# Two attention heads of one projection started in the same tick instead of two or four ticks apart

## The chip, the cores and the metric

The kernel runs on one core of one Trainium2 chip. The metric is the device time of one execution in microseconds (us). Before the change three runs gave 975.61, 977.11 and 977.17 us, median 977.11 us.

## What is computed

The reference is two transformer blocks for 256 tokens of width 1024, in float32. The first block has two layers: a multi-scale pooling mixer with a SwiGLU feed-forward, then a **differential attention** with eight heads (two score matrices per head, 64 wide, whose softmaxes are subtracted) with another SwiGLU. The second block has a mixer with three branches and a squared-ReLU feed-forward. Two of its branches are attentions with eight heads of width 64, called MoBA and DSA here; the third is a recurrent unit. DSA first lets an indexer select keys. Cut to the two attentions that matter:

```
s = einsum('bhcqd,bhckd->bhcqk', q, k) * 64**-0.5 + bias     # first block, c = 0, 1
p = softmax(where(rel >= 0, s, -inf))
o = (p[:, :, 0] - lam * p[:, :, 1]) @ v ; o = o * rsqrt(mean(o*o) + eps) * g
...
p = softmax(q @ k.T * 64**-0.5 + bias)                       # second block, heads a and b
y = p @ v
```

## The kernel before, in words

All instructions are emitted by one Python program, and each engine executes its own in the order in which they were emitted. A tile is taken from a pool when its first writer runs and goes back when its last reader has run. The pools of PSUM are small (`BANKS`, L169): four banks `acc`, two `mm`, two `tr`. If none is free, the writing instruction waits, and with it all that stands behind it on its engine.

The main work is projections and feed-forward products, split in high and low parts: each product is three matmuls (L318 to L320). A unit of weights (256 columns) comes by DMA as two raw tiles; ScalarE casts each to its high part (L92) and VectorE subtracts for the low part (L101). `Stream.step` emits these: two casts once a unit's room is released, and the subtractions one tick later.

Attention runs beside that work as Python generators in the list of `Side`. A call of `side.tick()` advances each generator by one step (until its next `yield`), in the order of the list, and then calls `Stream.step`. A generator may have a delay in ticks and a list of others that must have ended first. `proj_b` (L342) ticks after the first half of a unit (24 matmuls); `proj_t` (L816) copies the result from PSUM on ScalarE (L821, tile `qk`) after the second half and then ticks. So a projection is two ticks, an odd one in its middle and an even one at its end, and a pair of projections (q and k) is four. The casts of L92 come at even ticks behind the heads' instructions, the subtractions of L101 at odd ticks, also behind them.

The steps of one differential head (`diff_head`, L861, with `softmax`, L827), with letters used below:

- S: four score matmuls of 64 rows (L834) into two `acc` banks; VectorE adds the bias and reduces (L841, four instructions).
- E: four exponentials on ScalarE (L847).
- N: VectorE normalises and subtracts (L866 to L870).
- T: three transposes (L856) into one `tr` bank, copied out by ScalarE (L858).
- O: the value product, three matmuls (L877 to L879) into one `acc` bank; ScalarE squares (L883).
- G: two small instructions on GpSimd (L885, L388).
- D: VectorE scales out of the `acc` bank (L890).
- F: two transposes (L895) into one `tr` bank; ScalarE writes the high part from it (L314) and VectorE the low part from it (L315).

A pair of heads in the second block (`head_pair`, L1086) has six steps: S and E as above, N (L1091, L1094), T twice (six transposes in two `tr` banks, L856, with two copies L858), O (four matmuls of 64 columns, L1104, into one `acc` bank, high part by ScalarE, L1107) and the low part (L1109).

Before the change the eight differential heads are added two at a time after each q and k (L904 to L911): the first starts at the next tick, the second two ticks later. For the last pair the first head's S is run at once (L910), the second waits one tick. After them come the last part of v (`v_last`, L912: two ticks, with the copies L813 from its `mm` bank) and the output product (L914 to L923), whose first accumulators are both `mm` banks.

In the second block `heads_of` (L1116) adds two pairs of heads for MoBA at j = 0, the second four ticks after the first, and at j = 1 two more, each two ticks after the pair of j = 0 with its number has ended. They stand at the front of the list. DSA does the same later, after a masked bias is there. At the first tick of MoBA the indexer (L975) also runs a step, with four score matmuls in two times two `acc` banks.

Of the kernel before, what the change touches and what calls it, by code (L numbers as in the profile page):

```python
# [161 lines left out]
def model_kernel(ctx: ExitStack, tc: tile.TileContext, a: dict, out: bass.AP, stop=None):  # L162
# [16 lines left out]
    def gen(tag="rn", shape=(512,), dt=F32):  # L179
        return sb.tile([P] + list(shape), dt, tag=tag, name=nm(tag), bufs=BUFS[tag])  # L180
# [110 lines left out]
    side = Side(st)  # L291
# [85 lines left out]
    def hidden():  # L377
        return gen("hh", (2, 256), F32R), gen("hl", (2, 256), F32R)
# [427 lines left out]
    def v_last(v):  # L806
        u = st.take()[0]
        b = bank("mm")
        for t in range(2):
            proj_a(b[:, t * 256:(t + 1) * 256], t, u, False)  # L810
            if t:
                for i in range(2):
                    nc.scalar.copy(v[i][:, 768:1024], b[:, i * 256:(i + 1) * 256])  # L813
            side.tick()

    def proj_t():  # L816

        u = st.take()[0]
        b = proj_b(u)
        o = gen("qk", (2, 256))  # L820
        nc.scalar.copy(flat(o), b)  # L821
        side.tick()
        return o
# [79 lines left out]
    heads = []  # L903
    for j in range(4):  # L904
        qT, kT = proj_t(), proj_t()
        hts.append(hidden())
        for i in range(2):
            g = diff_head(qT, kT, i, 2 * j + i, hts[j], v, bias)
            if j == 3 and not i:
                next(g)  # L910
            heads.append(side.add(g, 2 * i if j < 3 else i))  # L911
    v_last(v)  # L912
    gb = bcast(a["ln_mix_g"][1]), bcast(a["ln_mix_b"][1])
    parts = list(zip(hts, st.take(4)))  # L914
# [171 lines left out]
    def head_pair(qT, kT, j, pr, b0, b1, v0, yT):  # L1086
        sx = []
        yield from softmax(qT, kT, j, lambda c, t: (b0, b1)[t](2 * pr + c), sx)
        p, sm = sx
        rc = small(4)  # L1090
        nc.vector.reciprocal(rc, sm)  # L1091
        for t in range(2):
            for c in range(2):
                nc.vector.tensor_scalar_mul(p[c][:, SPAN[t]], p[c][:, SPAN[t]], rc[:, 2 * t + c:2 * t + c + 1])  # L1094
        yield
        pT = [transpose3(p[c]) for c in range(2)]
        yield
        ob = bank("acc")
        for k in range(2):
            for c in range(2):  # L1100
                r = slice(c * 64, (c + 1) * 64)
                vc = slice(v0 + (2 * pr + c) * 64, v0 + (2 * pr + c + 1) * 64)
                q = slice(k * P, T)
                nc.tensor.matmul(ob[r, q], lhsT=v[k][:, vc], rhs=pT[c][:, (0, T)[k]:(T, 384)[k]],  # L1104
                                 start=k == 0, stop=k == 1, skip_group_check=True)
        h, l = yT[0][:, pr % 2], yT[1][:, pr % 2]
        nc.scalar.copy(h, ob[:, 0:T])  # L1107
        yield
        nc.vector.tensor_sub(l, ob[:, 0:T], h.bitcast(F32))  # L1109
# [6 lines left out]
    def heads_of(pairs, j, qT, kT, b0, b1, v0, yT, after=()):  # L1116

        for i in range(2):
            g = head_pair(qT, kT, i, 2 * j + i, b0, b1, v0, yT)
            pairs.append(side.add(g, 2 if j else 4 * i, pairs[i:i + 1] if j else after, True))  # L1120

    def moba(j):
        heads_of(ma, j, proj_t(), proj_t(), lambda h: bias_a[j][:, h % 4, P:T], lambda h: bias_a[j][:, h % 4], 0, yaT[j])

    def dsa(j, after):
        heads_of(d, j, proj_t(), proj_t(), lambda h: bias0[0][:, h], lambda h: bias_b[j][:, h % 4], 512, ybT[j], after)
# [19 lines left out]
    for what, j in MERGE:  # L1146
        u = st.take()[0]
        if what in "ABC":
            b = proj_b(u)
            g = gates[what, j] = gen("gt")  # L1150
# [12 lines left out]
        else:  # L1163
# [3 lines left out]
            g = gates.pop((what.upper(), j))  # L1167
# [60 lines left out]
def build(inputs, stop=None):  # L1228
    import concourse.bacc as _bacc

    nc = _bacc.Bacc("TRN2", target_bir_lowering=False, num_devices=1)
    arrays, args = {}, {}
    for name, v in [(n, inputs[n]) for n in _INS] + list(_constants().items()):
        v = np.ascontiguousarray(v)
        arrays[f"in_{name}_dram"] = v
        args[name] = nc.dram_tensor(f"in_{name}_dram", v.shape, mybir.dt.from_np(v.dtype), kind="ExternalInput").ap()
    out = nc.dram_tensor("out_0_dram", (1, T, D), F32, kind="ExternalOutput").ap()
    with tile.TileContext(nc) as tc:
        model_kernel(tc, args, out, stop)
    return nc, arrays  # L1240
# [8 lines left out]
```

## Time and profile before

| | us |
|---|---|
| runs, median (lowest to highest) | 977.11 (975.61 to 977.17) |
| the profiled execution, its own time | 977.19 |
| its span in the profile | 975.4 |
| TensorE busy | 951.4 (98%) |
| VectorE busy | 597.2 (61%) |
| ScalarE busy | 490.5 (50%) |
| GpSimd busy | 21.6 (2%) |
| chain of waits that ended last: TensorE's share | 89% |

The profile follows one execution. The difference of 1.8 us between its time and its span lies before the first and after the last instruction. TensorE is PE in the rows (PEld its weight loads), VectorE DVE, ScalarE ACT, GpSimd POOL. Matmuls are pipelined, so the time that one takes from the stream is read from start to start, not from its duration. A float32 matmul leaves two records.

### The profile page before, as it was taken

The numbers are of one execution on the slowest core, as the hardware profiler recorded it, in microseconds if no ns is written. First come the engines' busy times: TensorE is split into PE (matmuls) and PEld (weight loads), VectorE is DVE, ScalarE is ACT, GpSimd is POOL, SyncE is SP. The second block draws the span as 40 slices with busy tenths as digits, with TensorE's granted clock in tenths as the row PEclk, the third lists the DMA queues.
The fourth block names the chain that finished last, engine by engine and source line by source line (L and its number), as shares of the span: only waits on it lengthen the run. The fifth ranks groups of instructions, "written<-read, shape, count | busy, mean of one in ns | idle before, by whom it ended". The sixth has DMA issues, their size and how long they took to land.

```text
span 975.4 us, 16057 instructions
## 1 busy us (share of the span) xinstructions
PE 951.4 (98%) x6443; PEld 859.2 (88%) x6443; DVE 597.2 (61%) x985; ACT 490.5 (50%) x813; POOL 21.6 (2%) x44
## 2 busy tenths in 40 slices
PE   6999999999999999999998999999999999999997
PEld 5789999988998789999996999998999978898896
DVE  5774554466676864544458468958755676555454
ACT  3553543345666653433445456669644555344441
POOL 0000000000012000000001000000000000000000
PEclk9999999999999999999999999999999999999999
DMA  6576666556635466676752855443655657565531
GB/s 218 173 257 206 219 212 219 174 163 197 200 130 173 142 204 194 216 251 206 266 180 86 243 180 173 149 125 118 194 172 187 223 172 220 184 221 194 177 108 43
DMA packets 133939, 179.71 MB, mean 184 GB/s; under 512 B 8387, under 2 KB 114140, under 8 KB 133864
## 3 DMA queue, kind: packets, MB, share of 16 engines
q1 hardware_dynamic: 133008, 177.82, 57.0%
q8 instruction: 50, 0.82, 0.3%
q10 hardware_dynamic: 856, 0.87, 0.3%
q14 instruction: 25, 0.20, 0.1%
HBM read 177.51 MB, written 5.79 MB: 188 GB/s over the span
## 4 chain that ended last, share of the span: by engine, by line
PE 89%; DVE 5%; ACT 2%; issue 2%; DMA 1%; POOL 0%; POOLq 0%; DVEq 0%; ACTq 0%
PE mm L318 21%; PE mm L320 20%; PE mm L319 20%; PE acc L320 8%; PE acc L318 8%; PE acc L319 7%; DVE wl L101 2%; PE acc L834 1%; PE acc L1104 1%; PE tr L856 1%; DVE x L412 1%; ACT rn L401 1%; DMA bc<-in_pool_scale_dram 1%; PE tr L396 0%; POOL sm L388 0%
## 5 line engine op out<-in xcount | busy, mean ns | idle before, releaser
L101 DVE TENSOR_TENSOR wl<-raw,wh 128x1024 fp32r<-128x1024 f32 (+1 forms) x314 | 355.1, 1174 | 125.7 <-ACT wh L92 125.4
L92 ACT CAST wh<-raw 128x1024 fp32r<-128x1024 f32 (+1 forms) x314 | 303.2, 1012 | 171.5 <-issue 137.4
L318 PE MATMUL mm<-XTh,wh 128*128 128x256 f32 x1320 | 374.7, 284 | 0.0
L319 PE MATMUL mm<-XTl,wh 128*128 128x256 f32 x1320 | 368.2, 279 | 0.0
L320 PE MATMUL mm<-XTh,wl 128*128 128x256 f32 x1320 | 368.1, 279 | 0.0
L318 PEld LDWEIGHTS mm<-XTh,wh 128*128 128x128 f32 x1320 | 246.7, 187 | 5.9 <-issue 4.0
L319 PEld LDWEIGHTS mm<-XTl,wh 128*128 128x128 f32 x1320 | 247.7, 188 | 1.4
L320 PEld LDWEIGHTS mm<-XTh,wl 128*128 128x128 f32 x1320 | 248.2, 188 | 0.0
L318 PE MATMUL acc<-wh,hh 128*128 128x512 f32 x350 | 139.3, 398 | 0.0
L320 PE MATMUL acc<-wh,hl 128*128 128x512 f32 x350 | 139.0, 397 | 0.0
L319 PE MATMUL acc<-wl,hh 128*128 128x512 f32 x350 | 137.8, 394 | 0.0
L320 PEld LDWEIGHTS acc<-wh,hl 128*128 128x128 f32 x350 | 65.7, 188 | 16.5 <-DVE hl L312 0.4
L319 PEld LDWEIGHTS acc<-wl,hh 128*128 128x128 f32 x350 | 65.7, 188 | 14.4
L318 PEld LDWEIGHTS acc<-wh,hh 128*128 128x128 f32 x350 | 65.7, 188 | 13.7 <-ACT hh L311 0.2
L319 PE MATMUL mm<-wl,XTh 128*128 128x512 f32 (+1 forms) x144 | 53.7, 373 | 1.8 <-DVE wl L101 1.8
L318 PE MATMUL mm<-wh,XTh 128*128 128x512 f32 (+1 forms) x144 | 54.4, 378 | 0.2 <-ACT XTh L311 0.2
L320 PE MATMUL mm<-wh,XTl 128*128 128x512 f32 (+1 forms) x144 | 53.3, 370 | 0.3 <-DVE XTl L312 0.3
L312 DVE TENSOR_TENSOR hl<-rn,hh 128x512 fp32r<-128x512 f32 x30 | 20.8, 692 | 50.1 <-ACT hh L311 50.1
L605 ACT ACTIVATE rn<-mm 128x512 f32<-128x512 f32 x18 | 10.8, 602 | 60.7 <-PE mm L320 60.7
L821 ACT COPY qk<-mm 128x512 f32<-128x512 f32 x22 | 12.9, 588 | 44.0 <-PE mm L320 41.3
L319 PEld LDWEIGHTS mm<-wl,XTh 128*128 128x128 f32 x144 | 27.1, 188 | 8.1 <-DVE wl L101 3.6
L388 POOL TENSOR_TENSOR sm<-sm,mhalf 128x1 f32<-128x1 f32 (+1 forms) x22 | 14.4, 655 | 810.7 <-DVE sm L424 422.6
(208 smaller groups left out, 888.8 us busy)
## 6 DMA issues: line engine op xcount, KB each, us to landing
raw<-in_w_down_dram SPq DMA_DIRECT2D x76, 512.0 KB, 4.5
raw<-in_w_up_dram SPq DMA_DIRECT2D x68, 512.0 KB, 4.2
raw<-in_w_in_dram SPq DMA_DIRECT2D x60, 512.0 KB, 4.6
raw<-in_w_gate_dram SPq DMA_DIRECT2D x36, 512.0 KB, 4.4
raw<-in_w_qkv_dram SPq DMA_DIRECT2D x24, 512.0 KB, 3.6
raw<-in_w_o_dram SPq DMA_DIRECT2D x16, 512.0 KB, 3.7
Rd<-R SPq DMA_DIRECT2D x6, 766.0 KB, 7.0
raw<-in_w_gate_dram SPq DMA_DIRECT2D x16, 256.0 KB, 6.0
```

The source lines that it names most:

```text
L92: self.nc.scalar.copy(h, raw)
L101: self.nc.vector.tensor_sub(l, raw, h)
L312: nc.vector.tensor_sub(l, src, h.bitcast(F32))
L318: nc.tensor.matmul(o, lhsT=lh, rhs=rh, start=first, stop=False)
L319: nc.tensor.matmul(o, lhsT=lh, rhs=rl, start=False, stop=False)
L320: nc.tensor.matmul(o, lhsT=ll, rhs=rh, start=False, stop=last)
L388: nc.gpsimd.tensor_tensor(r2, v, mhalf.to_broadcast([P, n]) if n > 1 else mhalf, ALU.pow)
L401: nc.scalar.activation(gen(shape=(x.shape[-1],)), x, AF.Square, bias=bias, scale=1.0 / 32.0, accum_out=acc_col)
L412: nc.vector.scalar_tensor_tensor(x[:, c], x[:, c], ALPHA, mix, op0=ALU.mult, op1=ALU.add, accum_out=sums[:, h:h + 1])
L605: nc.scalar.activation(s, b, AF.Silu)
L821: nc.scalar.copy(flat(o), b)
L834: nc.tensor.matmul(bs[c][:, SPAN[t]], lhsT=qT[r, j, t * P:(t + 1) * P], rhs=kT[r, j, 0:P * (t + 1)], start=True, stop=True)
```

## The change

In the first block all heads start with delay 0, and for the last q and k both heads run S at once. In the second block both pairs of j = 0 start with delay 0, and both of j = 1 two ticks after both pairs of j = 0 have ended. No instruction is added or removed; only the order changes.

```diff
         for i in range(2):
             g = diff_head(qT, kT, i, 2 * j + i, hts[j], v, bias)
-            if j == 3 and not i:
+            if j == 3:
                 next(g)
-            heads.append(side.add(g, 2 * i if j < 3 else i))
+            heads.append(side.add(g))
     v_last(v)
...
         for i in range(2):
             g = head_pair(qT, kT, i, 2 * j + i, b0, b1, v0, yT)
-            pairs.append(side.add(g, 2 if j else 4 * i, pairs[i:i + 1] if j else after, True))
+            pairs.append(side.add(g, 2 if j else 0, pairs[0:2] if j else after, True))
```

## Rows read from the trace of the kernel before

**Rows 1.** Busy time by engine in the two attention stretches: PE, PEld, DVE, ACT, POOL, clock, DMA.

```profile
245.00:325.00 80.00, 78.63 (x592) 70.88 (x591) 61.20 (x188) 52.51 (x147) 9.45 (x16) 1.00 0.51 166
560.00:705.00 145.00, 143.09 (x1196) 134.28 (x1195) 110.05 (x267) 98.87 (x206) 0.74 (x2) 1.00 0.51 157
```

**Rows 2.** Timeline of PE around the first heads' S: start, us, engine, line, tiles, count.

```profile
251.01 0.28 PE L320 MATMUL mm<-XTh,wl 128*128 128x256 f32 x1
251.21 0.93 PE L834 MATMUL acc<-qk,qk 64*128 64x128 f32 x8
...
252.29 0.28 PE L319 MATMUL mm<-XTl,wh 128*128 128x256 f32 x1
...
257.93 0.93 PE L834 MATMUL acc<-qk,qk 64*128 64x128 f32 x8
```

**Rows 3.** Timeline of PE where a head pair's S meets the indexer.

```profile
578.61 0.93 PE L834 MATMUL acc<-qk,qk 64*128 64x128 f32 x8
579.36 0.60 PE L975 MATMUL acc<-at,qk 64*128 64x256 f32 x4
580.47 0.70 PE L975 MATMUL acc<-at,qk 64*128 64x256 f32 x4 [0.51 <-DVE sm L841]
```

**Rows 4.** Timeline of PE: a head pair's O behind another's S, and an O alone.

```profile
593.29 0.93 PE L834 MATMUL acc<-qk,qk 64*128 64x128 f32 x8
...
594.95 0.39 PE L318 MATMUL mm<-XTh,wh 128*128 128x256 f32 x1
...
701.62 0.87 PE L1104 MATMUL acc<-at,bc 128*64 128x256 f32 x8
702.42 0.39 PE L318 MATMUL mm<-XTh,wh 128*128 128x256 f32 x1
```

**Rows 5.** Timeline of DVE behind the first S: its first reduction, then the subtractions.

```profile
252.17 0.29 DVE L841 CUSTOM_DVE_ANT_0 at<-acc,bias 128x128 f32<-128x128 f32 x1 [2.83 <-PE acc L834]
...
253.29 2.36 DVE L101 TENSOR_TENSOR wl<-raw,wh 128x1024 fp32r<-128x1024 f32 x2
```

**Rows 6.** Timeline of DVE: one head's N, first and last instruction, and one F.

```profile
257.58 0.18 DVE L866 RECIPROCAL sm<-sm 128x4 f32<-128x4 f32 x1 [1.26 <-ACT at L847]
...
258.90 0.48 DVE L870 SCALAR_TENSOR_TENSOR at<-at,sm,at 128x256 f32<-128x256 f32 x1
...
278.38 0.48 DVE L315 SCALAR_TENSOR_TENSOR hl<-tr,sg,hh 128x256 fp32r<-128x256 f32 x1 [0.57 <-ACT hh L314]
```

**Rows 7.** Timeline of ACT: an even tick's copy, the first of one head's E, the casts.

```profile
255.20 0.59 ACT L821 COPY qk<-mm 128x512 f32<-128x512 f32 x1 [4.23 <-PE mm L320]
255.69 0.41 ACT L847 ACTIVATE at<-at,sm 128x128 f32<-128x128 f32 x1
...
257.46 1.98 ACT L92 CAST wh<-raw 128x1024 fp32r<-128x1024 f32 x2
```

**Rows 8.** Timeline of ACT: copies of one pair's T, a table load, the recurrent unit.

```profile
590.39 0.87 ACT L858 COPY at<-tr 128x384 f32<-128x384 f32 x2
...
614.19 1.09 ACT L1023 ACTIVATE rn<-qk,rnn 128x256 f32<-128x256 f32 x2
...
650.25 1.28 ACT L847 ACT_TABLE_LOAD   x1
...
680.98 1.15 ACT L1081 ACTIVATE hh<-qk 128x512 fp32r<-128x512 f32 x2
```

**Rows 9.** Timeline of PE: two waits of the kernel before in these stretches.

```profile
311.29 0.30 PE L856 MATMUL tr<-ident,at 128*128 128x128 f32 x1 [0.85 <-DVE at L870]
...
674.40 1.24 PE L1104 MATMUL acc<-at,bc 128*64 128x256 f32 x8 [0.95 <-ACT at L858]
```

**Rows 10.** Clock after an early wait of PE: timeline of PE, then two windows as in Rows 1.

```profile
17.20 3.64 PE L723 MATMUL acc<-pw,rn 128*128 128x256 f32 x8 [2.33 <-DVE rn L718]
...
17.40:20.70 3.30, 3.30 (x9) 2.45 (x9) 1.54 (x3) 1.10 (x2) 0.15 (x1) 0.50 0.07 24
20.80:30.00 9.20, 7.18 (x37) 5.82 (x36) 7.96 (x12) 4.86 (x6) 0.00 (x0) 1.00 0.46 142
```

## The prediction, made before the changed kernel ran

> **What bounds the kernel.** I read the busy times first: TensorE works 98% of the span, and in the two stretches that the change touches it is busy 78.6 of 80 us and 143.1 of 145 us [rows 1]. So what it does there, and what it would newly wait for, is the time. VectorE is busy 61.2 and 110.1 us of the same stretches, ScalarE 52.5 and 98.9 [rows 1]: two thirds to three quarters, which leaves little for work that comes in bursts. Then I read TensorE's timeline, to price each step of a head from start to start, and last the timelines of VectorE and ScalarE, to see in which order they serve the heads and the weights.
>
> Prices. Between the matmuls that frame S alone pass 1.28 us (251.01 to 252.29), two plain steps among them; from this S to the next pass 6.72 us, 48 plain steps and one S [rows 2]. Both together give a plain step of 0.118 us and an S of 1.04 us. A half projection, 24 steps, is 2.83 us, and two ticks are 5.7 us. The profiled execution took 977.19 us, 0.08 above the median of the runs; I add to the median. About 0.2% (2 us) is what a measurement tells from no change.
>
> **Part 1, what the joins save.** Where other matmuls of 64 rows follow S, they start 0.75 us after it [rows 3], not after the exit that makes S alone cost 1.04. A second S behind a first should cost a little less than 0.75, since its weights are loaded in the shadow of the first: I take 0.66, a gain of 0.38 per join (0.29 by the plain row). Four joins of differential heads: **-1.5**.
> In the second block an S and an O that stand together cost 1.85 us (593.29 to 594.95, and 0.2 at the edges), an O alone 1.0 (701.62 to 702.42, and 0.2) [rows 4]; an O behind an O should be 0.65, like an S. Four pairs before: S, three times S with O, O, so 1.04 + 5.55 + 1.0 = 7.6. After: twice two S (1.70) and two O (1.65), 6.7. Twice -0.9: **-1.8**.
> The rule of the Trainium skill that bears on it is in "TensorEngine Tiling (Array Packing)", Key Properties: a change of tiling mode drains TensorE, so that neighbours of one mode gain. The rows agree, with 0.75 against 1.04. By that rule alone all of the change would be gain, the first rival below.
>
> **Part 2, two S in four `acc` banks.** For the first and the last q and k all four banks are free. For the two between, the order of one tick becomes O, O, S, S: the two O hold a bank each until D, two ticks later, the first S takes the other two, and the second S has none until VectorE has reduced the first. The reductions start 0.96 us after S does (251.21 to 252.17) and take 1.12 (252.17 to 253.29) [rows 2, 5], so the bank is free 2.1 to 2.2 us after the first S began, where the second could have begun at 0.75 [rows 3]. TensorE executes in order: the next half projection stands behind. Two waits of 1.5 with the new entry: **+3.0**. That it waits so is seen where the indexer meets S: 0.51 us until the reduction [rows 3].
>
> **Part 3, F and T in two `tr` banks.** At the end of the second and of the third q and k the order of one tick becomes F, F, T, T (before, F and T of one head each, which just fits). Each F fills a bank that goes back when VectorE has written the low part. Count from x, the end of TensorE's projection at the tick of E. ScalarE: 0.2 until the copy, copy 0.5 (255.20 to 255.69), two E of 1.77 (255.69 to 257.46) [rows 7], so 4.25. The second N starts 0.1 later and takes 1.8 (257.58 to 259.38) [rows 6]: 6.15. Behind it on VectorE stand the tick's two subtractions, 2.36 [rows 5], and only then F's low part, 0.48 [rows 6]: x + 9.0. TensorE arrives after two half projections and the two F (four transposes at the plain step): x + 6.15. The wait is 2.85, twice: **+5.7**. What hid this before is that one head's E, N and F lay two ticks from the other's.
> The first pair's second T waits for its N (x + 6.15 against 5.7 + 0.35): **+0.2**. At the end of the first block the copies of v (L813) come behind two O, two E, and hold the bank that the output product's second half wants: my estimate is **+0.5**. The wait of the last head's T, 0.85 [rows 9], goes: **-0.9**.
>
> **Part 4, four T in two `tr` banks.** Two pairs in step make four T in a tick; the third waits for ScalarE's copy of the first. ScalarE: 0.2, copy 0.5, two E 3.54, the tick's casts 1.98 [rows 7], the next copy of q or k 0.5, one T copied 0.5 (0.87 for two) [rows 8]: x + 7.2. TensorE is there at 5.7 + 0.7. So the bare wait is 0.8; it grows by what else ScalarE does in these two ticks. MoBA first: a table load, 1.28 [rows 8], and the indexer's own work, which is late by about 0.5: 2.6. MoBA second: the recurrent unit's 1.09 [rows 8]: 1.9. DSA first: a table load and about 1 us of the recurrent unit: 3.0. DSA second: 1.15 [rows 8]: 1.9. Together **+9.4**. At MoBA's first tick the indexer, which took two banks freely and two after a wait, now waits for all four: **+0.7**. The wait of O at 674.40, 0.95 [rows 9], goes, since its T are far ahead: **-1.0**.
>
> **The sum.** First block -1.5 + 3.0 + 5.7 + 0.2 + 0.5 - 0.9 = +7.0. Second block -1.8 + 9.4 + 0.7 - 1.0 = +7.3. So 977.1 + 14.3 = 991.4 us, without the clock.
> **The clock.** TensorE's granted clock is 1.00 in both stretches [rows 1]. Early in the run it waited 2.33 us for VectorE, and from then on 0.50 was granted (1.2 of 2.4 GHz) for at least 3.3 us, before 1.00 again [rows 10]. Four of my waits are longer than 2.33 (2.85 twice, 2.6 and 3.0). Half speed for 3.3 us loses up to 1.65; I take 1.5. A fall after two of the four: +3.0, **994.4 us**. The Trainium skill, "TensorE: Matmul & The Clock Gate", in its table "Why this matters for your kernels", asks to avoid idle gaps between bursts of matmuls; by its limit none of my waits is long enough, and the sum would stay 991.4. The early wait speaks against it, and the page is not followed.
> No row of before shows eight such waits in these ticks. From below, the longest wait that it does show there is 0.95 [rows 9]: eight of that are 7.6 in place of 18.1, and the time 981. From above, waits longer by a sixth (+3.0) and four falls (+6.0): 1001. I take the worked-out waits, as the chains are made of measured pieces.
>
> **Rivals.** *Faster, the joins alone.* If the banks come back before TensorE asks (F's low part by x + 6.15 in place of x + 9.0, the T copies by x + 6.4), only the gains stay: -1.5 - 0.9 - 1.8 - 1.0 = -5.2, so 971.9. For it: each join gains by the rows. Against it: VectorE alone would need both the subtractions and a quarter of N out of the way. It decides where a burst of two E is shorter than about 2.3 us in place of 3.5.
> *Shorter waits.* If the casts are not behind the E of these ticks (no room in the weight buffers), the four T waits lose up to 2.0 each and all but vanish, -7.4, and there are fewer falls: 984. Against it: casts follow E in the row [rows 7].
> *No fall of the clock*: 991.4.
> *It does not do what it says.* In two of the four joins of differential heads the two S do not meet in time, because of the bank; that is in the sum.
>
> **Chances.** Forecast 0.50; no fall 0.20; shorter waits 0.18; joins alone 0.08; gains and waits that cancel 0.04. The range 981 to 1001 takes in all but the last two. Faster by over 0.2%: 0.08; within: 0.04; slower: 0.88.
>
> **What would show it.** In the changed profile: eight clusters of S of about 1.7 us, but with a wait on L841 inside two of the differential heads'; in front of T, TensorE idle for VectorE at L315 twice, near 2.6 us, and for ScalarE at L858 four times, 1 to 3 us; VectorE and ScalarE busy as long as before; TensorE's share of busy time down to about 97%; two to four stretches of granted clock 0.50 behind these waits. I am wrong if the waits on L315 and L858 are under 1 us each.

## The result: 992.29 us, and the profile after

The changed kernel takes 992.29 us (median; 991.51 to 993.82), against 977.11 before: a ratio of 1.0164, 95% interval 1.0153 to 1.0175, +15.2 us. The forecast was 994.4, with a range of 981 to 1001. The profiled execution took 992.13 us, its span is 990.3.

Where the time came from is read by three matmuls that stand outside the changed stretches and serve as anchors. L674 runs ahead of the first attention, L962 between the two, and the last of L396 behind the second. The fences give, for each line's matmuls, shape and count, min/median/max duration in ns, and the first and last start in us. First the kernel before:

```profile
L674 PE MATMUL tr<-ident,gt x1: 242/242/242, 239.5 to 239.5; 32*128 32x32 f32 x1
L962 PE MATMUL tr<-ident,at x2: 226/226/226, 564.1 to 564.1; 72*128 72x72 f32 x2
L396 PE MATMUL tr<-ident,rn x32: 270/273/328, 518.3 to 794.9; 128*128 128x128 f32 x32
```

And after:

```profile
L674 PE MATMUL tr<-ident,gt x1: 242/242/242, 237.8 to 237.8; 32*128 32x32 f32 x1
L962 PE MATMUL tr<-ident,at x2: 226/226/226, 570.1 to 570.1; 72*128 72x72 f32 x2
L396 PE MATMUL tr<-ident,rn x32: 270/273/329, 524.3 to 809.8; 128*128 128x128 f32 x32
```

L674 comes 1.7 us earlier, L962 6.0 later, the last transposes 14.9 later. So the start, which the change doesn't touch, gave 1.7 back in this execution (more on that at the end). **The first attention costs +7.7, the second +8.9**, 16.6 together. These two parts are quoted below for every kernel, always as differences to the profile of before.

Now the two stretches after (columns as in [rows 1]), and what TensorE waited for in them (total us, times, longest):

```profile
PE 954.1 (96%) x6443; PEld 863.6 (87%) x6443; DVE 597.5 (60%) x985; ACT 491.3 (50%) x813; POOL 19.1 (2%) x44
...
245.00:335.00 90.00, 82.23 (x593) 73.83 (x591) 62.57 (x188) 54.12 (x152) 7.53 (x17) 0.98 0.48 153
570.00:722.00 152.00, 143.13 (x1177) 134.85 (x1177) 109.34 (x266) 98.00 (x206) 0.74 (x2) 0.98 0.47 141
```

```profile
PE tr L856 <- DVE hl L315: 5.2, 2, 2.6
PE acc L834 <- DVE sm L841: 1.9, 2, 0.9
PE mm L318 <- ACT bc L813: 0.7, 1, 0.7
...
PE tr L856 <- ACT at L858: 8.2, 4, 3.6
PE acc L975 <- DVE sm L841: 0.3, 1, 0.3
PE tr L856 <- DVE at L1094: 0.2, 1, 0.2
```

The first three are the first attention, the rest the second. All but the last 0.2 are waits for a PSUM bank, in the tiles and on the lines that the prediction named; the four for L858 last 3.6, 2.1, 1.6 and 0.9 us, where 1 to 3 was forecast. VectorE and ScalarE are as busy as before (597 and 491 us): no work was added, only waiting. The idle times in these rows sum to 16.5 us.

The two kinds of wait in the first attention, in TensorE's timeline (start, us, then the instruction, and in brackets the idle time before it and its releaser; a transpose leaves one record, so that x6 is the T of two heads and x4 the F of two):

```profile
249.45 1.58 PE L834 MATMUL acc<-qk,qk 64*128 64x128 f32 x16
...
264.63 0.93 PE L834 MATMUL acc<-qk,qk 64*128 64x128 f32 x8
266.50 1.26 PE L834 MATMUL acc<-qk,qk 64*128 64x128 f32 x8 [0.94 <-DVE sm L841]
276.30 0.60 PE L895 MATMUL tr<-ident,at 128*128 128x128 f32 x4
279.53 1.54 PE L856 MATMUL tr<-ident,at 128*128 128x128 f32 x6 [2.64 <-DVE hl L315]
...
297.46 0.60 PE L895 MATMUL tr<-ident,at 128*128 128x128 f32 x4
300.65 0.94 PE L856 MATMUL tr<-ident,at 128*128 128x128 f32 x6 [2.60 <-DVE hl L315]
```

At 249.45, with all `acc` banks free, two S stand in one piece of 1.6 us. At 264.63 two O hold two banks, and the second S stands apart. At 276.30 F fills both `tr` banks and T stops. What held those two banks is seen on VectorE and ScalarE (same columns):

```profile
276.33 0.48 DVE L870 SCALAR_TENSOR_TENSOR at<-at,sm,at 128x256 f32<-128x256 f32 x1
276.73 2.35 DVE L101 TENSOR_TENSOR wl<-raw,wh 128x1024 fp32r<-128x1024 f32 x2
279.00 0.87 DVE L315 SCALAR_TENSOR_TENSOR hl<-tr,sg,hh 128x256 fp32r<-128x256 f32 x2
```

```profile
274.85 1.98 ACT L92 CAST wh<-raw 128x1024 fp32r<-128x1024 f32 x2
...
277.21 0.83 ACT L314 ACTIVATE hh<-tr,sg 128x256 fp32r<-128x256 f32 x2
```

F's low part (L315) stands behind the subtractions (L101), and these behind the second head's N (L870, ended at 276.8). L101 started when N was over and ran 2.35 us. ScalarE's share of F (L314), behind the casts, ends at 278.0, a microsecond before L315 starts, so it is VectorE that holds the banks. The chain is the one that the prediction counted, link by link.

The longest wait is the third of the four in the second attention:

```profile
665.09 0.82 PE L856 MATMUL tr<-ident,at 128*128 128x128 f32 x6
669.49 1.54 PE L856 MATMUL tr<-ident,at 128*128 128x128 f32 x6 [3.58 <-ACT at L858]
...
671.48 0.41 PE L318 MATMUL mm<-XTh,wh 128*128 128x256 f32 x1
671.69 0.41 PE L319 MATMUL mm<-XTl,wh 128*128 128x256 f32 x1
```

```profile
660.24 1.28 ACT L847 ACT_TABLE_LOAD   x1
661.53 0.40 ACT L847 ACTIVATE at<-at,sm 128x128 f32<-128x128 f32 x1
...
665.06 0.49 ACT L1054 ACTIVATE rn<-rn,sp 128x256 f32<-128x256 f32 x1
665.47 0.49 ACT L1055 ACTIVATE rn<-rn,sp 128x256 f32<-128x256 f32 x1
665.87 0.49 ACT L1056 ACTIVATE rn<-rn,sp 128x256 f32<-128x256 f32 x1
666.26 1.12 ACT L92 CAST wh<-raw 128x512 fp32r<-128x512 f32 x2
667.29 0.51 ACT L1054 ACTIVATE rn<-rn,sp 128x256 f32<-128x256 f32 x1
...
668.50 0.58 ACT L1151 ACTIVATE gt<-mm 128x512 f32<-128x512 f32 x1
668.98 0.84 ACT L858 COPY at<-tr 128x384 f32<-128x384 f32 x2
```

T was in its banks at 665.9, but its copy (L858) stands behind the table load, eight exponentials, six activations of the recurrent unit, a cast and a gate. The granted clock (the third column from the end) fell within this wait and within the first one for L315:

```profile
279.00:282.00 3.00, 2.47 (x12) 2.47 (x13) 0.87 (x3) 1.32 (x3) 0.00 (x0) 0.50 0.80 294
...
668.00:674.00 6.00, 4.51 (x21) 4.51 (x22) 1.16 (x3) 5.22 (x12) 0.00 (x0) 0.50 0.48 134
```

Two falls to 0.50 (1.2 of 2.4 GHz), as forecast; both are there before TensorE resumes, at 279.53 and 669.49. In the second, a plain step lasts 0.21 (671.48 to 671.69), where it takes 0.118 otherwise.

### The profile page after: what moved, and what is told of

Its sections match the earlier page's. It is cut to its first block, busy times and chain, and to the rows that moved or that the text cites. A ratio compares the mean times of both kernels' runs of the same rounds, so it can differ in the third digit from the quotient of the medians.

```text
span 990.3 us, 16064 instructions
## 1 busy us (share of the span) xinstructions
PE 954.1 (96%) x6443; PEld 863.6 (87%) x6443; DVE 597.5 (60%) x985; ACT 491.3 (50%) x813; POOL 19.1 (2%) x44
## 4 chain that ended last, share of the span: by engine, by line
PE 62%; ACT 3%; DVE 2%; issue 1%; POOL 0%; POOLq 0%; ACTq 0%; DVEq 0%
PE mm L318 14%; PE mm L320 14%; PE mm L319 14%; PE acc L320 6%; PE acc L318 6%; PE acc L319 6%; ACT at L847 1%; PE acc L1104 1%; PE tr L856 1%; PE acc L834 1%; ACT wh L92 1%; DVE wl L101 0%; PE tr L396 0%; PE tr L1039 0%; PE acc L975 0%
## 5 line engine op out<-in xcount | busy, mean ns | idle before, releaser
L101 DVE TENSOR_TENSOR wl<-raw,wh 128x1024 fp32r<-128x1024 f32 (+1 forms) x314 | 355.1, 1174 | 130.6 <-ACT wh L92 130.2
L318 PE MATMUL mm<-XTh,wh 128*128 128x256 f32 x1320 | 375.2, 284 | 0.0
L318 PEld LDWEIGHTS mm<-XTh,wh 128*128 128x128 f32 x1320 | 248.1, 188 | 5.0 <-issue 3.1
L318 PE MATMUL acc<-wh,hh 128*128 128x512 f32 x350 | 139.1, 398 | 0.0
L318 PEld LDWEIGHTS acc<-wh,hh 128*128 128x128 f32 x350 | 65.7, 188 | 13.9 <-ACT hh L311 0.2
L318 PE MATMUL mm<-wh,XTh 128*128 128x512 f32 (+1 forms) x144 | 54.9, 381 | 0.2 <-ACT XTh L311 0.2
L318 PEld LDWEIGHTS mm<-wh,XTh 128*128 128x128 f32 x144 | 27.4, 190 | 5.4 <-ACT XTh L311 0.5
```

Source lines behind the costliest of these rows:

```text
L101: self.nc.vector.tensor_sub(l, raw, h)
L318: nc.tensor.matmul(o, lhsT=lh, rhs=rh, start=first, stop=False)
```

## The experiments

Theory: the cost is waits for `acc` and `tr` banks, which come back late because two heads' bursts stand in one queue; the joins themselves gain. Rival: heads in step cost TensorE time in other ways too (late softmaxes, queues), so that other banks would not bring it back. Eight kernels were run.

**1 and 2. Each hunk alone.** Kernel 1 changes the differential heads only, kernel 2 the head pairs only:

```diff
-            if j == 3 and not i:
+            if j == 3:
                 next(g)
-            heads.append(side.add(g, 2 * i if j < 3 else i))
+            heads.append(side.add(g))
```

```diff
-            pairs.append(side.add(g, 2 if j else 4 * i, pairs[i:i + 1] if j else after, True))
+            pairs.append(side.add(g, 2 if j else 0, pairs[0:2] if j else after, True))
```

> The change in the first block alone (heads in step), the second block as before. Theory (waits for banks): the first block's part of the trace, from its first S to the transposes behind it, was 7.7 us longer than before, so 984.8 us (983 to 986.5), with the two waits for L315 and the two for L841 as in the changed kernel, and one fall of the clock or none. Rival (the two halves work on each other, through weights that come late): another time than the sum allows, under 982 or over 988.

> The change in the second block alone. Theory: 15.2 less 7.7 is 7.5, by the trace up to 9.0, so 985.3 us (984 to 987), with four waits for L858 of 1.8 to 3.6 us and a fall of the clock behind the longest. Rival (the halves work on each other): under 982 or over 988.

Measured: 985.97 us (ratio 1.0083, 1.0056 to 1.0109) and 987.43 (1.0102, 1.0077 to 1.0127). By the anchors, hunk 1 costs +7.7 in the first attention, hunk 2 +9.3 in the second, where the full change has 7.7 and 8.9. So the two hunks don't act on each other as far as the anchors tell: 17.0 in sum against 16.6. The medians alone are too wide to say so (+8.4 and +9.8, each uncertain by about 2.6, against +15.2). Kernel 1 came out as expected; kernel 2 lies 0.4 above its range. It again had a fall of the clock within its longest wait.

**3. Other banks for F.** The change, with F's two transposes in `acc`:

```diff
-        tb = bank("tr")
+        tb = bank("acc")
         for t in range(2):
             c = slice(t * P, (t + 1) * P)
             nc.tensor.transpose(tb[:, c], o[:, c], ident)
```

> The changed kernel, but F of the differential heads takes its bank from acc, which are free in that tick, in place of tr. Theory (T waits because F's readers hold the tr banks): the two waits for L315, 2.6 to 2.9 us each, go, and the fall of the clock behind the first (about 1.4); at the last q and k the second S now waits for an acc bank that F holds, about 1.7 us. 992.3 - 5.6 - 1.4 + 1.7 = 987.0 us (985 to 989). Rival (two heads in step make VectorE late, and the wait only moves): T waits for N instead, as long, 991 to 993.

Measured: 988.35 us (1.0111, 1.009 to 1.0132). The first attention costs +2.4 in place of +7.7, a gain of 5.3, as expected. TensorE's waits there are now:

```profile
PE acc L834 <- DVE sm L841: 1.9, 2, 0.9
PE acc L834 <- DVE hl L315: 1.1, 1, 1.1
PE mm L318 <- ACT bc L813: 0.7, 1, 0.7
```

T no longer waits there, and no fall follows. L315 is as late as before: the last pair's S now meets it, since F has its `acc` banks. So the bank, not the length of VectorE's queue alone, decides who waits.

The second attention, whose code is that of the change, costs +7.9 here in place of +8.9. Its four waits are the same, but the clock fell elsewhere: the longest wait, 3.58 us, was not followed by half clock, and a fall came behind the one of 2.09 us at 597.05. TensorE, then the two windows:

```profile
668.03 0.92 PE L856 MATMUL tr<-ident,at 128*128 128x128 f32 x6 [3.58 <-ACT at L858]
```

```profile
597.00:601.00 4.00, 3.95 (x22) 3.89 (x23) 3.83 (x11) 3.12 (x5) 0.00 (x0) 0.62 0.49 142
668.00:674.00 6.00, 5.97 (x53) 5.31 (x54) 2.35 (x3) 5.38 (x12) 0.00 (x0) 1.00 0.34 112
```

**4. Other banks for T.** The change, with the second transposes of every pair in `acc`, so that four T have four banks:

```diff
-    def transpose3(src):
+    def transpose3(src, tag="tr"):
...
-        tb = bank("tr")
+        tb = bank(tag)
...
-        pT = [transpose3(p[c]) for c in range(2)]
+        pT = [transpose3(p[c], ("tr", "acc")[c]) for c in range(2)]
```

> The changed kernel, but in the second block the second T of a pair takes its bank from acc, so that four T of a tick have four banks. Theory (the third T waits for ScalarE to empty a bank): the four waits for L858, 8.2 us together, go, with the long fall of the clock (about 3); O, one tick later, waits for copies that are late, 1 to 2 us in all. 992.3 - 8.2 - 3 + 1.5 = 982.6 us (980.5 to 985). Rival (ScalarE is late whatever the bank, and the wait only moves to O): 989 to 993.

Measured: 986.06 us (1.0091, 1.0069 to 1.0113), above the range by 1.1. The second attention costs +1.4 in place of +8.9, and all four waits for L858 are gone. But another wait, 0.2 us in the full change, is now 1.2 us long in front of the last T, and the clock fell behind it. VectorE first, then TensorE, then the window behind:

```profile
687.94 0.69 DVE L1077 SCALAR_TENSOR_TENSOR qk<-rn,qk 128x512 f32<-128x512 f32 x1
688.66 0.69 DVE L1078 TENSOR_TENSOR qk<-qk,rn 128x512 f32<-128x512 f32 x1
...
690.60 1.28 DVE L101 TENSOR_TENSOR wl<-raw,wh 128x512 fp32r<-128x512 f32 x2
...
692.01 1.01 DVE L1094 TENSOR_SCALAR at<-at,sm 128x128 f32<-128x128 f32 x4
```

```profile
692.36 0.90 PE L856 MATMUL tr<-ident,at 128*128 128x128 f32 x3 [1.19 <-DVE at L1094]
```

```profile
694.00:698.00 4.00, 4.00 (x21) 4.00 (x22) 3.62 (x5) 3.33 (x6) 0.00 (x0) 0.57 0.34 118
```

N comes behind the recurrent unit's work and the subtractions. In the full change TensorE was late by the other waits when it came here, and these hid most of it. The first attention, whose code is that of the change, costs 6.6 here with the same waits (L315 5.3 us in two) and no fall of the clock, against 7.7 with one in two other executions. That prices this fall at **1.1 us**.

**5 to 8. All banks dealt out anew.** Kernel 5 has both hunks (only the early S of the last q and k is for the first head alone, as before) and T as in run 4, with

```diff
-        ob = bank("acc")
+        ob = bank("tr" if head < 4 else "acc")
...
-        tb = bank("tr")
+        tb = bank("acc" if head < 6 else "tr")
```

for O and F of the first attention. Kernel 6 has these two edits and the first hunk (early S as in 5), with the second attention as before. Kernel 8 has the two edits alone, with neither hunk. Kernel 7 is kernel 5 with MoBA's first pairs four ticks later:

```diff
-            pairs.append(side.add(g, 2 if j else 0, pairs[0:2] if j else after, True))
+            pairs.append(side.add(g, 2 if j else 0 if after else 4, pairs[0:2] if j else after, True))
```

> Both hunks of the change stay, except that the second head of the last q and k does not run its scores early; and the banks are dealt out another way: in the first block F of the first six heads takes acc banks and O of the first four takes tr banks, in the second block the second transposes of each pair take an acc bank. Theory: nearly all that the change costs is waits for a bank's release, so with those gone only the saving of the joins, the wait for the late normalisation at the last four transposes of the second block, and the indexer's 0.8 us are left. First-block part: with the F banks moved alone it was +2.35, of which 1.74 (scores of the last pair) and 3.07 (the two acc waits) should go now: -2.5, or about -1 if a third of the saving is eaten by waits not seen so far. Second-block part +1.45 as with the T banks moved alone (+0.3 if no clock fall follows). Sum -2 to +0.5 against before, 976.5 (975 to 978.5). Rival, that heads in step cost PE time beyond the bank waits (late softmaxes, the engines' queues): both parts stay positive and the time stays above 981.

> Only the first block is changed, with the banks as in the run above; the second block is that of before. Theory: the first-block part is -1 to -2.5, the second zero: 975.5 (974.5 to 977). TensorE's clusters with two heads' scores take about 1.7 and with two heads' value products about 1.65, without a wait for L841 or L315. Rival as above: 978 to 981, with new waits on E or N in the place of those for banks.

> As the first kernel of this call, but both pairs of the first MoBA projection start four ticks later, when the indexer has run its scores, and all that follows them moves with it. Theory: the indexer's +0.8 us goes; DSA's last four transposes, which waited 1.2 us for the recurrent unit's share of VectorE, move by four ticks too, so that wait and its clock fall change as well, by how much is open. Second-block part -2.3 to +1.5, the whole 975.5 (973.5 to 978). Rival: MoBA's outputs are now late for the gated products, which wait for them: second-block part above +2.

> Neither hunk, only the first block's banks dealt out as in the second kernel of this call: the control for it. Theory: the banks of before cost little (its gone waits are 0.9 us), so this is within 1 us of before: 977 (976 to 978.2), and the second kernel of this call is 1 to 2.5 us faster than this one, which is what joining the heads saves in the first block (4 x 0.38 predicted). Rival: the joins save nothing, the two are equal.

Measured, against 976.94 for before on the same chip:

| kernel | us, median | ratio (95% interval) | first attention | second attention |
|---|---|---|---|---|
| 5, both, all banks moved | 975.22 | 0.9984 (0.9976 to 0.9993) | -2.0 | +0.1 |
| 6, first joined, banks moved | 974.88 | 0.9980 (0.9970 to 0.9989) | -2.05 | -0.4 |
| 7, as 5, MoBA four ticks later | 974.77 | 0.9979 (0.9970 to 0.9988) | -2.0 | -0.5 |
| 8, banks alone | 977.70 | 1.0008 (1.0000 to 1.0016) | +0.7 | -0.1 |

All four lie within their ranges, and the rival falls: with the banks moved, TensorE waits for nothing in the joined part of the first attention. Kernel 6, from its timeline, in the same places as the fence of after (two S behind two O, and T behind two F):

```profile
264.59 1.58 PE L834 MATMUL acc<-qk,qk 64*128 64x128 f32 x16
274.69 0.60 PE L895 MATMUL acc<-ident,at 128*128 128x128 f32 x4
275.13 0.82 PE L856 MATMUL tr<-ident,at 128*128 128x128 f32 x6
```

Kernels 6 and 8 differ in the order alone: 974.88 against 977.70, and in the first attention -2.05 against +0.7. So heads in step, which cost 7.7 us in the old banks, gain 2.8 against this control, a little more than the 1 to 2.5 expected, and the banks alone gain nothing. Two things limit the comparison. The control's +0.7 is a wait that these banks cause in the old order (L318 waits 0.4 us of idle time for L315), so that 2.05, against before, is the gain without it. And in kernels 5 to 7 the last pair is one tick apart, as before: three pairs of heads are joined, not four.

In the second attention the differences say little: kernels 1 and 6, whose code there is that of before, show -0.4. So kernels 5 and 7 lose nothing there any more, and a gain isn't shown. The banks of the second attention were not run alone. Kernels 5 to 7 are faster than both the kernel before and the changed one (the latter timed in other runs), by about 0.2% and 1.7 to 1.8%; among them the intervals don't tell which is best. In kernel 7 the indexer's wait is gone, as expected, and the wait for N at the last T (1.2 us idle) stays in 5 and 7. That a later start of DSA would remove it wasn't tried.

## Why the prediction was right, step by step

| step | predicted | measured |
|---|---|---|
| first attention: joins, gone wait, first T | -2.2 | -2.05 (kernel 6, three joins of four) |
| two S waits in `acc` | +3.0 | +3.1 |
| two T waits in `tr`, for F | +5.7 | +6.5, some of it at half clock |
| copies of v | +0.5 | +0.9 (0.7 of it idle) |
| a fall of the clock | +1.5 | +1.1 (run 4) |
| second attention: four T waits | +9.4 | +10.7, some at half clock |
| indexer | +0.7 | +0.8 |
| joins and gone wait | -2.8 | -4.4, as the remainder |
| a fall, outside the T wait | +1.5 | +1.8 |

Measured waits are from start to start: a joined group's time from the plain step in front of it to the second one behind it, less that of the same group where nothing waits (OOSS 4.83 against 3.28 us in kernel 6, FFTT 4.91 against 1.33, TTTT 3.91, 3.42, 6.08 and 3.49 against 1.55 at best in kernel 5). The first attention's rows add to 9.55 where 7.7 was measured. The T row and the fall's row hold the same half-clock transposes (1.54 against 0.94 us, 0.6), and the first row lacks the fourth join (0.4); the rest, 0.85, is not resolved. The forecast's 8.5 for the same rows is thus nearer to the whole than to their sum.

That the second attention came out (8.8 forecast, 8.9 measured) is luck in part: the T waits were put 1.3 too small and the gain 1.6 too small, and these cancel.

**The joins.** Two S stand from 249.45 for 1.7 us with their edges, as forecast (1.70); two O take 1.65, as forecast. The O are those of the second attention, where two S take 1.70 as well; so the joins there are the -1.8 of the forecast. The other 2.6 of the -4.4 are not the joins': the O of [rows 9], whose idle time of 0.95 was 1.4 from start to start; 0.5 us that TensorE idled in front of L1039 before the change and no longer does; and 0.4 by which kernels 1 and 6 are shorter too, whose second attention is that of before. The last 0.3 is open.

**The acc banks.** 1.5 each, forecast and measured, and the releaser is L841.

**The tr banks, first attention.** The estimate of 2.85 was hit at 300.65 (2.9). At 279.53 the transposes behind the wait ran at half clock and it came to 3.6.

**The tr banks, second attention.** Three of four come out: 2.35, 1.9 and 1.9 (forecast 2.6, 1.9, 1.9). The last of them is luck in part: its idle time is 0.9 us for L858, under the 1 us that the prediction set as its sign of being wrong, and 0.2 for N (L1094); in kernel 5, where no T waits for L858, N alone made the same group take 3.92 us. **The third was mis-sized**: 3.0 against 4.5. The step allowed "a table load and about 1 us of the recurrent unit"; the table load was there, but six activations of the recurrent unit stood ahead of the copy, 2.4 us (665.06 to 666.26 and 667.29 to 668.50), and the transposes then ran at half clock. Run 3, where the clock stayed at 1.00 here, tells the two apart: the same group took 5.39 us, a wait of 3.8, so that 0.7 of the 4.5 is the clock.

**The clock.** Two falls, in the longest wait and in one of 2.64 us, at a price near the forecast. By the time alone the rival without a fall (991.4) would be nearer to 992.29 than the forecast is; the falls in the profile decide against it. That two falls came and not another number is luck, for the five runs' mean granted clock was 0.991 to 0.995. The premise, that the waits over 2.33 us are the ones that can bring a fall, was wrong in part: 2.64 us of idle time brought a fall, 2.60 us twenty microseconds later brought none (clock 1.00 from 300 to 304), and in run 4 the very same two waits brought none either, while 1.19 us at 692.36 was followed by one; the same 1.19 us before the last T of kernel 5 was not. In run 3 even 3.58 us brought none, where the same wait did in the full change and in run 2. So a wait of this size may be followed by half clock; a row of one execution doesn't say that it must. The Trainium skill, "TensorE: Matmul & The Clock Gate" (table "Why this matters for your kernels"), by whose limit none of the forecast waits was to bring a fall, is not borne out here. Falls came with idle times of 2.64 and 1.19 us, which are under its limit, and idle times of 3.57 to 3.58 us, which are over it, brought one in the full change and in run 2, and none in run 3.

The two stretches cost 16.6 us where the sum had 17.3. The forecast of 994.4 lies 2.1 above the result: 0.7 is this difference, and the rest is of the size of the start, 1.7 shorter in the profiled execution, which the change doesn't touch; that part is chance.

The rival *joins alone* (971.9) describes what happens when the banks come back in time: kernels 5 and 7 come to 975, as the wait for N (2.4 from start to start) and, in kernel 5, the indexer (0.8) keep some of it, and the last pair is not joined. That rival's limit of 2.3 us for two E does not follow from its figures: the bare T wait would need them at 2.7 in place of 3.5, F's wait at 0.7.

## What to carry to other kernels

Before two units of work are put in step, count the banks that are held in one tick, and follow each to its release through the other engines' queues: here heads in step gained 2.05 us with one allotment of banks and lost 7.7 with another, in which S waited for the reductions of the S before it and T for two banks that stood behind 2.35 us of subtractions. When such an order costs time, deal out the banks anew before giving it up, and run the banks alone as the control. Removed waits uncover those behind them (here N at the last T), so that the gain is read from the next profile, not from the sum of the waits.

## What was not expected of the hardware

The start of the kernel, the same code in all, differs between executions by up to 2.9 us (L674 at 237.7 to 240.6), and in the pair below the clock is most of the difference. In the profile of before 0.50 was granted early on [rows 10]; kernel 6 waited longer at the same place and kept 1.00:

```profile
17.13 1.99 PE L723 MATMUL acc<-pw,rn 128*128 128x256 f32 x8 [3.46 <-DVE rn L718]
...
17.00:21.00 4.00, 3.73 (x20) 3.02 (x20) 2.48 (x6) 2.83 (x6) 0.48 (x1) 1.00 0.15 49
```

The same eight matmuls take 1.99 us here and 3.64 in [rows 10], 1.65 more, and L674 comes 1.8 us earlier. So a median of a few runs of this kernel carries the luck of its start, which is as large as the gains of kernels 5 to 7; stretches between two anchors of the trace don't. They do carry the falls of the clock inside them: the second attention of the change cost 8.9, 9.3 and 7.9 us in the three executions that run its code unaltered (the full change, runs 2 and 3).
